# Forgetting attention as a list of steps, with its pieces at fixed places and TensorE in program order

## The chip, the cores and the metric

The kernel runs on one core of a Trainium2 chip. Its engines are TensorE (PE: matrix products; PEld is its weight load), VectorE (DVE), ScalarE (ACT), GpSimd (POOL) and SyncE (SP, which issues DMA transfers). The metric is the time of one execution on the device in microseconds; the figure before is a median of three runs.

## The reference

Two layers work on x of 512 rows by 1024 columns in float32. Each has a SwiGLU feed-forward, a mixer and another feed-forward, all on a normed x and added to it. The mixer of layer 0 is a gated linear recurrence (HGRN2), that of layer 1 the forgetting attention (FoX) of this case:

```
def fox_mixer(h, w_in, b_f, q_norm_g, k_norm_g, w_out):
    q, k, v, g, z_f = split(h @ w_in)              # 16 heads of 64 columns; z_f: one column for each head
    q = rmsnorm(q, q_norm_g);  k = rmsnorm(k, k_norm_g)   # over the 64 columns of a head
    c = cumsum(log_sigmoid(z_f + b_f), axis=rows)
    s = q @ k.T / sqrt(64) + c[query] - c[key]     # only keys at or before the query
    o = softmax(s) @ v
    return (o * sigmoid(g)) @ w_out
```

## The kernel before, in words

Every float32 product is three products: each operand is split into a high part and a rest (`split`, L148: a copy on ScalarE, a subtraction on VectorE), and `mm3` (L167) issues high by high, rest by high and high by rest, at lines 169 to 171. Weights arrive by DMA, are split, and are used once. PSUM has eight banks, given out by kind (L90).

The feed-forwards, and the output projections of both mixers, are written as lists of `Step` objects: a step has `early` work (loads and splits, with a lead in steps), `hooks` (work put ahead of its products), its products `mm`, and `post`. `Line.run` (L293) writes them out one after the other.

The forgetting attention is no such list. `fox` (L868 on) handles the 16 heads in four groups of four, each group as two pairs. For a group it writes, in this order: q and k for all rows (`proj_N`, 96 products of 128x512, tiles `xq..`) with the sums of squares for the norm; the root by a power on GpSimd (`rsqrt_cols`, L177) and the multiplication of q and k by it (`xn`, L998); the values (96 products of 128x256, `xv..`); the gate of the first pair (24 products, `xg..`); the turning of q and k of both pairs by TensorE transposes (`xtp`, L1014) into the stacks QH, QL and KS; the gate of the second pair; and then `attend` for either pair. In group 0 the values' products have 16 more columns, z_f; these are turned (`xzp`, L916) and become c, which goes to DRAM (`cd`) and comes back spread over 128 partitions (`cbc`). `attend` writes the scores for query tiles 3, 2, 1, 0 and both heads (`sc`, two products each, L944 and L945), each followed on VectorE by a pass that adds c and finds the row's extreme (L948), on ScalarE by Exp (L951), and on VectorE by the division (L952, L953). Its `rest` turns the probabilities back (`pT`, L965), copies them (L970 on VectorE, L968 on ScalarE), multiplies them with the values (`xo<-PP,xV`, L973) and applies the gate (L975).

The order in which an engine takes these instructions is not the written one. A scheduler lays the instructions of each engine in order, and puts products of the next group between the pieces of attention of the one before. The `rest` of the last pair is the `late` hook of the output projection, `steps_mix` (L586; xo_ for this mixer, ho_ for the recurrence), which starts when it is written.

Of the kernel before, what the change touches and what calls it, by code (L numbers as in the profile page):

```python
# [12 lines left out]
F32R = mybir.dt.float32r  # L13
# [31 lines left out]
def trunk(ctx: ExitStack, tc: tile.TileContext, a):  # L45
    nc = tc.nc
    MM = nc.tensor.matmul
# [131 lines left out]
    class Norm:  # L179
# [31 lines left out]
        def turn(self, j, kh, kind="turn"):  # L211
# [6 lines left out]
            for kp in range(2):  # L218
                pt = psum(f"{self.id}t{j}{kh}{kp}", (2, H), kind)
                for kk in range(2):  # L220
                    for t in range(2):
                        k = kp * 2 + kk
                        nc.tensor.transpose(pt[:, kk, t * P:(t + 1) * P], self.ys[kh * 2 + t][:, k * P:(k + 1) * P], ident)
# [361 lines left out]
    def steps_mix(nm, src, act, done, late):  # L585

        st = {"w": {}, "b": {}, "bank": {}}

# [9 lines left out]
        def split_b(q):  # L598
            st["b"][q] = split(act(q // 2, 0)[:, q % 2 * 2:q % 2 * 2 + 2, :], B_HL, [2, T], f"{nm}b{q}")

        def mm(half, q, ts, last):
            def what():
                h, l = st["w"]["hl", half, q]
                bh, bl = st["b"][q]
                for t, bank in ts:
                    if q == 0:
                        st["bank"][half, t] = psum(f"{nm}{half}{t}", bank=bank)
                    for kk in range(2):
                        mm3(st["bank"][half, t], bh[:, kk, t * P:(t + 1) * P], bl[:, kk, t * P:(t + 1) * P],
                            h[:, kk, :], l[:, kk, :], q == 0 and kk == 0, q == 3 and kk == 1)  # L610
                if last:
                    drop(bh, bl)
            return what

        def post(half, ts):
# [8 lines left out]
        steps = []  # L624
        for part, (half, ts) in enumerate(((0, ((0, 0), (1, 1), (2, 2))), (1, ((0, 3), (1, 4))),
                                           (1, ((2, 5), (3, 6))), (0, ((3, 7),)))):
            for q in range(4):
                s = Step()
                if part != 2:
                    s.early += [(8, lambda half=half, q=q, part=part: load(half, q, part)), (3, lambda half=half, q=q: split_w(half, q))]  # L630
                if part == 0 and q < 3:
                    s.early.append((3, lambda q=q: split_b(q)))
                elif part == 0:
                    s.hooks += [*late, lambda: split_b(3)]
                s.mm = mm(half, q, ts, part == 3)
                if q == 3:
                    s.post = post(half, ts)
                steps.append(s)
        return steps
# [52 lines left out]
    def hgrn(norm, act, parts):  # L692
# [91 lines left out]
        def states(pr, K, V, tot):  # L784
# [3 lines left out]
            for e in range(2):  # L788
                hs = slice(e * P, (e + 1) * P)
                pk = psum(f"hk{pr}{e}", (NT - 1, P), "ms")  # L790
                for c in range(NT - 1):
                    nc.tensor.transpose(pk[:, c, :], K[:, e, c * P:(c + 1) * P], ident)
# [38 lines left out]
        def finish(pr, ons, gs):  # L831
            for e in range(2):
                h = pr * 2 + e
                pt = psum(f"hot{h}", kind="ms")
                for t in range(NT):
                    nc.tensor.transpose(pt[:, t * P:(t + 1) * P], ons[e][:, t, :], ident)
# [25 lines left out]
    def fox(norm, act, parts):  # L862
        w_in = a["fox_w_in"][0]
        cd = dram.tile([FH, T], F32, name="cd")
        ar0 = turn_of["ar"]
        attended = [0]

# [17 lines left out]
        def values(gr):  # L885

            V = at("ar3", [NT, 256], f"xV{gr}")
            n = 256 + (FH if gr == 0 else 0)
            hs = []
            for q in range(2):  # L890
                w = at("w", [4, 256], f"xv{gr}{q}")
                nc.sync.dma_start(w, w_in[q * 512:(q + 1) * 512, 2 * D + gr * 256:2 * D + gr * 256 + 256].rearrange("(k p) c -> p k c", p=P))
                if gr:
                    hs.append(split(w, W_HL, [4, 256], f"xv{gr}{q}"))
                    drop(w)
                    continue
                h, l = (at("ar", [4, n], f"xv{x}{q}", F32R, slot=ar0 + 2 * q + i) for i, x in enumerate("hl"))
                for cs, raw in ((slice(0, 256), w), (slice(256, n), wz[:, 4 * q:4 * q + 4, :])):
                    nc.scalar.activation(h[:, :, cs], raw, AF.Copy)
                    nc.vector.tensor_sub(l[:, :, cs], raw, r32(h[:, :, cs]))  # L900
                drop(w)
                hs.append((h, l))
            zn = at("y", [NT, FH], "zn") if gr == 0 else None
            for c in range(NT):
                ts = slice(c * P, (c + 1) * P)
                pv = psum(f"xvp{gr}{c}", kind="mm")
                for k in range(NK):
                    h, l = hs[k // 4]
                    mm3(pv[:, :n], norm.cut("h", k, ts), norm.cut("l", k, ts), h[:, k % 4, :], l[:, k % 4, :], k == 0, k == NK - 1)
                nc.scalar.copy(V[:, c, :], pv[:, :256])  # L910
                if gr == 0:
                    nc.scalar.copy(zn[:, c, :], pv[:, 256:n])
            if gr == 0:
                pz = psum("xzp", kind="ms")
                for c in range(NT):
                    nc.tensor.transpose(pz[:FH, c * P:(c + 1) * P], zn[:, c, :], ident)  # L916
                forget(pz[:FH])
            return V

        def attend(gr, pr, stacks, V, sgT):  # L920
            QH, QL, KS = stacks[pr]
            cbs, PPs, sms, mns = [], [], [], []
            for par in range(2):
                h = gr * 4 + pr * 2 + par
                i = attended[0] % 3
                attended[0] += 1
                cb = at(("p1", "p1", "V2")[i], [T], f"cbc{h}", slot=(0, 1, 0)[i])
                nc.sync.dma_start(cb, cd[h:h + 1, :].partition_broadcast(P))
                cbs.append(cb)
                PPs.append(at("ar", [NT, NT, P], f"PP{h}", slot=ar0 + par))  # L930
                both = small(2 * NT, f"mn{h}")
                mns.append(both[:, :NT])
                sms.append(both[:, NT:])
# [3 lines left out]
            for t in reversed(range(NT)):  # L937
                W = (t + 1) * P
                ts_ = slice(t * P, W)
                for par in range(2):  # L940
                    h = gr * 4 + pr * 2 + par
                    cb, PP, mn = cbs[par], PPs[par], mns[par]
                    sc = psum(f"sc{h}{t}", kind="lv")
                    MM(sc[:, :W], lhsT=QH[:, par, ts_], rhs=KS[:, par, :W], start=True, stop=False)  # L944
                    MM(sc[:, :W], lhsT=QL[:, par, ts_], rhs=KS[:, par, :W], start=False, stop=True)  # L945
                    nc.gpsimd.tensor_add(cb[:, ts_], cb[:, ts_], cmask)  # L946
                    row = PP[:, 0:t + 1, t, :]
                    nc.vector.tensor_tensor_reduce(row, cb[:, :W].rearrange("p (b s) -> p b s", s=P),  # L948
                                                   sc[:, :W].rearrange("p (b s) -> p b s", s=P), 1.0, 3.0e38,
                                                   op0=ALU.add, op1=ALU.min, accum_out=mn[:, t:t + 1])  # L950
                    nc.scalar.activation(row, row, AF.Exp, scale=-1.0, bias=mn[:, t:t + 1], accum_out=sms[par][:, t:t + 1])  # L951
                    nc.vector.reciprocal(sms[par][:, t:t + 1], sms[par][:, t:t + 1])  # L952
                    nc.vector.tensor_scalar_mul(row, row, sms[par][:, t:t + 1])  # L953

            drop(QH, QL, KS)

            def rest():
                po = psum(f"xo{gr}{pr}", kind="po")
                for s in range(NT):
                    N = (NT - s) * P  # L960
                    for par in range(2):
                        h = gr * 4 + pr * 2 + par
                        pT = psum(f"pT{h}{s}", kind="ms")
                        for t in range(s, NT):
                            nc.tensor.transpose(pT[:, (t - s) * P:(t - s + 1) * P], PPs[par][:, s, t, :], ident)  # L965
                        PT = PPs[par][:, s, s:, :].rearrange("p t q -> p (t q)")
                        if par:
                            nc.scalar.copy(PT, pT[:, :N])  # L968
                        else:
                            nc.vector.tensor_copy(PT, pT[:, :N])  # L970
                    for par in range(2):
                        rows = slice(par * FD, (par + 1) * FD)
                        MM(po[rows, s * P:], lhsT=V[:, s, (pr * 2 + par) * FD:(pr * 2 + par + 1) * FD],  # L973
                           rhs=PPs[par][:, s, s:, :].rearrange("p t q -> p (t q)"), start=s == 0, stop=s == NT - 1)
                nc.vector.tensor_mul(head_tile(act, gr * 2 + pr), po, sgT[:, pr, :])  # L975
                if pr:
                    drop(sgT)
            return rest

        for gr in range(4):  # L980

            nat = [at("w", [NT, 256], f"xn{gr}{i}") for i in range(2)]
# [188 lines left out]
```

## Time and profile before

| | |
|---|---|
| median of three runs | 2011.36 us (2006.01 to 2011.91) |
| profiled execution | 2011.04 us, span 2009.2 us |
| granted TensorE clock, mean | 0.993 |
| TensorE busy | 1959.0 us, 97% of the span |
| VectorE, ScalarE, GpSimd busy | 1455.6, 1058.2, 261.2 us |
| DMA | 281.40 MB, mean 140 GB/s |

The forgetting attention and its output projection lie between 1342.94 and 1671.52 us of the span. An engine's busy time is the union of its instructions' times; neighbouring matmuls overlap in the trace, so what one costs is read from the distance between two starts.

### The profile page before, as it was taken

The numbers are of one execution on the slowest core, as the hardware profiler recorded it, in microseconds if no ns is written. First come the engines' busy times: TensorE is split into PE (matmuls) and PEld (weight loads), VectorE is DVE, ScalarE is ACT, GpSimd is POOL, SyncE is SP. The second block draws the span as 40 slices with busy tenths as digits, with TensorE's granted clock in tenths as the row PEclk, the third lists the DMA queues.
The fourth block names the chain that finished last, engine by engine and source line by source line (L and its number), as shares of the span: only waits on it lengthen the run. The fifth ranks groups of instructions, "written<-read, shape, count | busy, mean of one in ns | idle before, by whom it ended". The sixth has DMA issues, their size and how long they took to land.

```text
span 2009.2 us, 31752 instructions
## 1 busy us (share of the span) xinstructions
PE 1959.0 (97%) x12821; PEld 1754.9 (87%) x12821; DVE 1455.6 (72%) x1848; ACT 1058.2 (53%) x1595; POOL 261.2 (13%) x249
## 2 busy tenths in 40 slices
PE   6999999999999999999999999999999899999999
PEld 5999987888888899998799999878767668999987
DVE  6767798466565977789797678975566559777796
ACT  6554565432233754556464546567466647444553
POOL 1111211000000011111101110112212200111111
PEclk9999999999999999999999999999999999999999
DMA  6767887221123476785847678672232323767865
GB/s 172 175 154 164 203 186 182 83 63 64 53 85 116 107 178 157 158 227 135 205 110 163 158 162 225 140 176 74 69 91 82 117 63 102 176 154 158 223 149 141
DMA packets 253938, 281.40 MB, mean 140 GB/s; under 512 B 12192, under 2 KB 196944, under 8 KB 253792
## 3 DMA queue, kind: packets, MB, share of 16 engines
q1 hardware_dynamic: 190144, 203.48, 32.3%
q0 software_dynamic: 60576, 75.51, 23.8%
q8 instruction: 100, 1.64, 0.3%
q10 hardware_dynamic: 3072, 0.39, 0.1%
q14 instruction: 46, 0.38, 0.1%
HBM read 277.21 MB, written 2.13 MB: 139 GB/s over the span
## 4 chain that ended last, share of the span: by engine, by line
PE 41%; DVE 4%; ACT 3%; DMA 1%; issue 1%; POOL 0%; POOLq 0%; DVEq 0%; ACTq 0%; SPq 0%
PE f10op L169 2%; PE f10op L170 2%; PE f11op L169 2%; PE f10op L171 2%; PE f11op L170 2%; PE f11op L171 2%; PE xo L973 1%; PE pT L965 1%; PE xvp L171 1%; PE xvp L170 1%; PE xvp L169 1%; PE xo L169 1%; PE xo L171 1%; PE xo L170 1%; DMA f11u4r<-in_ffn_w_in_dram 1%
## 5 line engine op out<-in xcount | busy, mean ns | idle before, releaser
L375 ACT ACTIVATE act<-act 128x512 f32<-128x512 f32 x60 | 37.6, 627 | 55.8 <-DVE act L405 48.5
L946 POOL TENSOR_TENSOR cbc<-cbc,cmask 128x128 f32<-128x128 f32 x64 | 31.6, 496 | 162.4 <-DVE mn L948 112.1
L970 DVE COPY PP<-pT 128x512 f32<-128x512 f32 (+3 forms) x32 | 15.7, 491 | 38.4 <-PE pT L965 38.4
L755 PEld LDWEIGHTS lv<-Q,K 128*128 128x128 f32 x320 | 37.7, 192 | 3.5 <-issue 2.9
L755 PE MATMUL lv<-Q,K 128*128 128x64 f32 x320 | 38.7, 273 | 0.0
L951 ACT ACTIVATE PP<-PP,mn 128x512 f32<-128x512 f32 (+3 forms) x64 | 35.4, 557 | 5.5 <-DVE mn L948 5.0
L965 PEld LDWEIGHTS pT<-ident,PP 128*128 128x128 f32 x160 | 17.7, 145 | 21.6 <-issue 13.4
L968 ACT COPY PP<-pT 128x512 f32<-128x512 f32 (+3 forms) x32 | 13.6, 425 | 40.7 <-PE pT L965 40.7
L948 DVE CUSTOM_DVE_ANT_0 PP<-cbc,sc 128x256 f32<-128x256 f32 (+3 forms) x64 | 30.6, 482 | 6.0 <-PE sc L945 2.9
L165 POOL DMA_DIRECT2D f01ox<-in_ffn_w_out_dram x18 | 20.5, 1143 | 110.0 <-DVE f01op70l L156 31.7
L165 POOL DMA_DIRECT2D f11ox<-in_ffn_w_out_dram x18 | 20.5, 1140 | 107.7 <-DVE f11op70l L156 30.1
L165 POOL DMA_DIRECT2D f00ox<-in_ffn_w_out_dram x18 | 20.4, 1138 | 107.7 <-DVE f00op L472 32.0
L165 POOL DMA_DIRECT2D f10ox<-in_ffn_w_out_dram x18 | 20.5, 1154 | 106.4 <-DVE f10op L472 32.6
L973 PE MATMUL xo<-PP,xV 128*64 128x512 f32 (+3 forms) x128 | 30.8, 467 | 0.0
L944 PE MATMUL sc<-KS,QH 128*128 128x512 f32 (+3 forms) x64 | 23.0, 361 | 7.8 <-DVE mn L948 5.1
L765 DVE TENSOR_TENSOR Q<-Q,tot 128x512 f32<-128x512 f32 x24 | 16.6, 692 | 16.7 <-PE lv L755 10.7
L965 PE MATMUL pT<-ident,PP 128*128 128x128 f32 x160 | 26.7, 294 | 1.3 <-DVE PP L953 1.2
L944 PEld LDWEIGHTS sc<-KS,QH 128*128 128x128 f32 x64 | 12.4, 194 | 16.6 <-DVE mn L948 8.5
L953 DVE TENSOR_SCALAR PP<-PP,mn 128x512 f32<-128x512 f32 (+3 forms) x64 | 25.2, 404 | 1.0
L998 DVE TENSOR_TENSOR xn<-xn,xrr 128x1024 f32<-128x1024 f32 x8 | 9.4, 1223 | 21.3 <-POOL xrr L177 21.3
L945 PE MATMUL sc<-KS,QL 128*128 128x128 f32 (+3 forms) x64 | 21.5, 338 | 0.5 <-ACT QL L1023 0.5
L973 PEld LDWEIGHTS xo<-PP,xV 128*64 128x64 f32 x128 | 9.6, 137 | 13.0 <-DVE PP L970 10.5
(5442 smaller groups left out, 8613.5 us busy)
## 6 DMA issues: line engine op xcount, KB each, us to landing
f00op<-in_ffn_w_out_dram SPq DMA_DIRECT2D x20, 512.0 KB, 4.7
f01op<-in_ffn_w_out_dram SPq DMA_DIRECT2D x20, 512.0 KB, 4.6
f10op<-in_ffn_w_out_dram SPq DMA_DIRECT2D x20, 512.0 KB, 4.6
f11op<-in_ffn_w_out_dram SPq DMA_DIRECT2D x20, 512.0 KB, 4.5
f00ox<-in_ffn_w_out_dram POOLq DMA_DIRECT2D x15, 512.0 KB, 7.8
f01ox<-in_ffn_w_out_dram POOLq DMA_DIRECT2D x15, 512.0 KB, 8.4
f10ox<-in_ffn_w_out_dram POOLq DMA_DIRECT2D x15, 512.0 KB, 7.1
f11ox<-in_ffn_w_out_dram POOLq DMA_DIRECT2D x15, 512.0 KB, 8.3
```

The source lines that it names most:

```text
L165: nc.gpsimd.dma_start(out, in_, accum_op=ALU.add)
L169: MM(out, lhsT=lh, rhs=rh, start=first, stop=False, skip_group_check=more)
L170: MM(out, lhsT=lh, rhs=rl, start=False, stop=False, skip_group_check=more)
L171: MM(out, lhsT=ll, rhs=rh, start=False, stop=last, skip_group_check=more)
L375: nc.scalar.activation(out, out if make else it["A"], AF.Silu)
L755: MM(pl[:, c], lhsT=Kc[:, c, :], rhs=Qv[:, c, :, 1, :], start=True, stop=True)
L944: MM(sc[:, :W], lhsT=QH[:, par, ts_], rhs=KS[:, par, :W], start=True, stop=False)
L946: nc.gpsimd.tensor_add(cb[:, ts_], cb[:, ts_], cmask)
L948: nc.vector.tensor_tensor_reduce(row, cb[:, :W].rearrange("p (b s) -> p b s", s=P), sc[:, :W].rearrange("p (b s) -> p b s", s=P), 1.0, 3.0e38,
L951: nc.scalar.activation(row, row, AF.Exp, scale=-1.0, bias=mn[:, t:t + 1], accum_out=sms[par][:, t:t + 1])
L965: nc.tensor.transpose(pT[:, (t - s) * P:(t - s + 1) * P], PPs[par][:, s, t, :], ident)
L973: MM(po[rows, s * P:], lhsT=V[:, s, (pr * 2 + par) * FD:(pr * 2 + par + 1) * FD], rhs=PPs[par][:, s, s:, :].rearrange("p t q -> p (t q)"), ...
```

## The change

The attention becomes `steps_fox`: 32 steps for each group (16 of q and k, 8 of values, 8 of gates), with loads and splits at a fixed lead. All mixers and feed-forwards from the recurrence's output projection on are one `Line`. The attention of a pair is cut into seven pieces: scores of tile 3, of tile 2, of tiles 1 and 0; then the turning of s=0, that of s=1 with the product of s=0, that of s=2 and 3 with the product of s=1, and the products of s=2 and 3 with the gate. Two more pieces for a group turn q and k of either pair. A table, `PLACES`, names for each piece the step ahead of which it is put, and from the first step of the attention to the middle of the output projection every TensorE instruction is kept in program order. The output projection is cut into smaller steps, for both mixers.

```
+    pe_in_order = [False]
+
+    def MM(*args, **kw):
+        ins = nc.tensor.matmul(*args, **kw)
+        if pe_in_order[0]:
+            tc.keep_in_program_order(ins)
...
+            def rest0():
+                turn(0)
+            def rest1():
+                turn(1)
+                weigh(0)
+            def rest2():
+                turn(2, 3)
+                weigh(1)
+            def rest3():
+                weigh(2)
+                weigh(3)
...
+            return [scores(3), scores(2), scores(1, 0), rest0, rest1, rest2, rest3]
+        return [s for gr in range(4) for s in group(gr)], turned, attend
...
+    fox, turned, attend = steps_fox(n4, act)
+    fox[0].hooks += [lambda: pe_in_order.__setitem__(0, True), lambda: n4.scaled(1)]
...
+    xo, second, split_last = steps_mix("xo_", a["fox_w_out"][0], act, feed(n5), [])
+    xo[second].hooks.append(lambda: pe_in_order.__setitem__(0, False))
+    mid = fox + xo
+    PLACES = (((20, 28), (32, 34, 36, 38, 40, 41, 42), (43, 45, 47, 50, 52, 53, 54)),
...
+    for gr, (turns, *pairs) in enumerate(PLACES):
+        for pr in range(2):
+            mid[turns[pr]].hooks.append(lambda gr=gr, pr=pr: turned(gr, pr))
+            for n, what in zip(pairs[pr], attend(gr, pr)):
+                mid[n].hooks.append(what)
...
-    Line(xo + s3 + o3).run()
+    Line(ho + s1 + o1 + s2 + o2 + fox + xo + s3 + o3).run()
```

On TensorE, the turn of q and k of the last group: `xvp` are values' products, `xg30p` those of the gate of the first pair, `xtp` the transposes. Before, it stands behind all 96 products of values and the 24 of the gate:

```order
L171 MATMUL xvp_15116<-xv31h,n11l_12756 128x256
L169 MATMUL xg30p<-n11h_12749,xg30h 128x512
...
L171 MATMUL xg30p<-n11h_12752,xg30l 128x512
L1014 MATMUL xtp_15180<-ident,xn_14868 128x128 x4
L1014 MATMUL xtp_15193<-ident,xn_14869 128x128 x4
L169 MATMUL xg31p<-n11h_12749,xg31h 128x512
```

After, it stands behind the first 36 products of values:

```order
L50 MATMUL xqp_14958<-xq33sh,n11l_12765 128x512
L50 MATMUL xvp_15023<-xv03sh,n11h_12758 128x256
...
L50 MATMUL xvp_15050<-xv03sh,n11l_12763 128x256
L55 MATMUL xtp_15066<-ident,xn_14815 128x128 x4
L55 MATMUL xtp_15079<-ident,xn_14816 128x128 x4
L50 MATMUL xvp_15050<-xv13sh,n11h_12760 128x256
```

The transposes have moved ahead of 60 products of values and the 24 of the gate; `xqp` is the last product of q and k, from which `xn` is made.

On VectorE, the end of the second pair of group 0: `PP<-pT` are the copies of the turned probabilities (the last two of four are shown), `xn` the multiplication of the next group's q and k by the root, `xss` and `xr1v` what that waits for. Before:

```order
L970 COPY PP_13501<-pT_13598 128x256
L992 TENSOR_REDUCE xss_13619<-xs_13735 128x8
L970 COPY PP_13501<-pT_13608 128x128
L975 TENSOR_TENSOR act_13497<-xo_13571,sgT_13269 128x512
L156 TENSOR_TENSOR xv10l<-xv_13775,xv10h 128x1024
L156 TENSOR_TENSOR xv11l<-xv_13781,xv11h 128x1024
L156 TENSOR_TENSOR xg10l<-xg10w,xg10h 128x1024
L992 TENSOR_REDUCE xss_13619<-xs_13765 128x8
L176 TENSOR_SCALAR xr1v<-xss_13619 128x32
L156 TENSOR_TENSOR xg11l<-xg11w,xg11h 128x1024
L998 TENSOR_TENSOR xn_13617<-xn_13617,xrr_13768 128x1024
L998 TENSOR_TENSOR xn_13618<-xn_13618,xrr_13768 128x1024
```

After:

```order
L166 TENSOR_TENSOR xg11sl<-xg_13800,xg11sh 128x1024
L1142 RECIPROCAL mn_13624<-mn_13624 128x1
L186 TENSOR_SCALAR xr1v<-xss_13483 128x32
L1168 COPY PP_13619<-pT_13771 128x512
L1143 TENSOR_SCALAR PP_13623<-PP_13623,mn_13624 128x128
L1009 TENSOR_TENSOR xn_13481<-xn_13481,xrr_13738 128x1024
L1009 TENSOR_TENSOR xn_13482<-xn_13482,xrr_13738 128x1024
L1168 COPY PP_13619<-pT_13815 128x384
L1168 COPY PP_13619<-pT_13841 128x256
L1168 COPY PP_13619<-pT_13842 128x128
```

The two `xn` have moved from behind all four copies of the probabilities to between the first and the second; a split (`xg11sl`) and two rows of the softmax (`mn`, `PP_13623`) stand ahead of them.

On ScalarE, the Exp of the first pair of group 1. Before, from the gate's Sigmoid (`sgT`) of the second pair on:

```order
L1005 ACTIVATE sgT_13895<-xg11p 128x512
L1023 ACTIVATE QL_13927<-QL_13927 64x512
L155 ACTIVATE xq2s3h<-xq2w_14266 128x1024
L1019 ACTIVATE QH_13951<-xtp_13954,cols 64x512
L1020 ACTIVATE QH_13951<-xtp_13954,cols 64x512
L1025 ACTIVATE KS_13953<-xtp_13967,cols 64x512
L951 ACT_TABLE_LOAD
L951 ACTIVATE PP_14008,mn_14009<-PP_14008,mn_14009 128x4x128
```

After:

```order
L165 ACTIVATE xq22sh<-xq_13972 128x1024
L1141 ACTIVATE PP_13983,mn_13984<-PP_13983,mn_13984 128x4x128
L1141 ACTIVATE PP_13987,mn_13988<-PP_13987,mn_13988 128x4x128
L1054 ACT_TABLE_LOAD
L1054 ACTIVATE sgT_14097<-xgp_13931 128x512
L1141 ACT_TABLE_LOAD
L1141 ACTIVATE PP_13983,mn_13984<-PP_13983,mn_13984 128x3x128
```

One Sigmoid of the gate, which stood ahead of the softmax, stands inside it now, with a table load on either side.

## Rows read from the trace of the kernel before

**Rows 1.** Page, busy time, share of the span and instructions of an engine
```profile
PE 1959.0 (97%) x12821; PEld 1754.9 (87%) x12821; DVE 1455.6 (72%) x1848; ACT 1058.2 (53%) x1595; POOL 261.2 (13%) x249
```
**Rows 2.** Windows: stretch, length, busy of PE, PEld, DVE, ACT, POOL, then clock
```profile
1342.94:1392.54 49.60, 49.36 (x271) 42.06 (x270) 22.93 (x33) 28.25 (x53) 7.17 (x2) 1.00 0.14 42
1392.54:1459.66 67.12, 65.66 (x361) 50.11 (x360) 40.12 (x97) 41.31 (x85) 15.66 (x20) 1.00 0.28 85
1459.66:1526.45 66.79, 65.47 (x361) 50.12 (x360) 40.00 (x97) 41.05 (x85) 14.39 (x17) 1.00 0.32 95
1526.45:1592.81 66.36, 65.09 (x360) 49.71 (x358) 40.61 (x98) 40.74 (x84) 14.30 (x17) 1.00 0.33 104
1592.81:1671.52 78.71, 71.44 (x321) 50.81 (x320) 51.49 (x112) 45.88 (x88) 8.56 (x15) 0.91 0.29 83
```
**Rows 3.** Waits of PE, 1342.94 to 1671.52: total, times, longest (us)
```profile
PE sc L944 <- DVE mn L948: 5.1, 6, 1.5
```
**Rows 4.** Timeline of PE: start, length, engine, line, operation, tiles, shape
```profile
1434.99 0.39 PE L171 MATMUL xq1p<-xq1s3h,n11l 128*128 128x512 f32 x1
...
1435.67 0.39 PE L171 MATMUL xq1p<-xq1s3h,n11l 128*128 128x512 f32 x1
...
1436.01 0.28 PE L170 MATMUL xvp<-xv10l,n11h 128*128 128x256 f32 x1
1436.13 0.28 PE L171 MATMUL xvp<-xv10h,n11l 128*128 128x256 f32 x1
```
**Rows 5.** Timeline of PE, products with the values and transposes of one s
```profile
1409.33 1.35 PE L973 MATMUL xo<-PP,xV 128*64 128x512 f32 x4
1410.62 0.87 PE L965 MATMUL pT<-ident,PP 128*128 128x128 f32 x6
```
**Rows 6.** Timeline, the norm of group 1's q and k
```profile
1436.63 0.62 ACT L991 ACTIVATE xs<-xq1p 128x512 f32<-128x512 f32 x1
...
1438.32 6.42 POOL L177 TENSOR_TENSOR xrr<-xr1v,cols 128x32 f32<-128x32 f32 x1 [12.27 <-ACT xg11h L155]
1444.77 2.36 DVE L998 TENSOR_TENSOR xn<-xn,xrr 128x1024 f32<-128x1024 f32 x2 [5.33 <-POOL xrr L177]
```
**Rows 7.** Timeline, from group 1's turn to its first turned probabilities
```profile
1452.88 1.03 PE L1014 MATMUL xtp<-ident,xn 128*128 128x128 f32 x8
...
1455.71 0.67 ACT L1019 ACTIVATE QH<-xtp,cols 64x512 fp32r<-64x512 f32 x1
...
1461.79 1.06 ACT L155 ACTIVATE xq2s3h<-xq2w 128x1024 fp32r<-128x1024 f32 x1
...
1462.88 1.23 DVE L156 TENSOR_TENSOR xq2s3l<-xq2w,xq2s3h 128x1024 fp32r<-128x1024 f32 x1 [0.65 <-ACT xq2s3h L155]
...
1464.84 1.28 ACT L951 ACT_TABLE_LOAD   x1
...
1466.13 0.72 ACT L951 ACTIVATE PP<-PP,mn 128x512 f32<-128x512 f32 x1
...
1474.63 1.09 PE L965 MATMUL pT<-ident,PP 128*128 128x128 f32 x8 [0.15 <-DVE PP L953]
```
**Rows 8.** Windows, the same stretch (columns as in rows 2)
```profile
1455.71:1474.63 18.92, 17.61 (x82) 13.14 (x80) 14.24 (x40) 18.42 (x38) 2.93 (x6) 1.00 0.36 112
```
**Rows 9.** Timeline, from z_f to the first use of c
```profile
1380.38 0.28 PE L916 MATMUL xzp<-ident,zn 128*16 128x128 f32 x1
...
1393.03 0.46 POOL L946 TENSOR_TENSOR cbc<-cbc,cmask 128x128 f32<-128x128 f32 x1 [16.61 <-DMA cbc<-cd]
```
**Rows 10.** Timeline of PE around a wait in a feed-forward
```profile
986.76 0.40 PE L171 MATMUL f01op<-f01op55h,f01obp52l 128*128 128x512 f32 x1
990.40 0.80 PE L169 MATMUL f01op<-f01op30h,f01obp30h 128*128 128x512 f32 x1 [3.23 <-DVE X L526]
```
**Rows 11.** Windows, behind that wait, and in the last block
```profile
1600.00:1613.80 13.80, 9.62 (x24) 5.12 (x25) 10.32 (x27) 11.22 (x24) 1.86 (x4) 0.51 0.07 24
990.40:996.00 5.60, 5.60 (x13) 4.46 (x14) 3.94 (x4) 2.33 (x6) 1.31 (x1) 0.50 0.07 14
```

More of the change, by code (lines that the diff above doesn't have):

```diff
@@ L596, in split_w, with split_b, mm @@
             drop(w)
[L598 to L601 removed]
+        def split_b(q, kk=None):
+            if q not in st["b"]:
+                st["b"][q] = at(B_HL[0], [2, T], f"{nm}b{q}h", F32R), at(B_HL[1], [2, T], f"{nm}b{q}l", F32R)
+            cut = slice(0, 2) if kk is None else slice(kk, kk + 1)
+            h, l = (x[:, cut, :] for x in st["b"][q])
+            raw = act(q // 2, 0)[:, q % 2 * 2:q % 2 * 2 + 2, :][:, cut, :]
+            nc.scalar.activation(h, raw, AF.Copy)
+            nc.vector.tensor_sub(l, raw, r32(h))
+        def mm(part, q, ts, kks, first, last):
+            half = parts[part][0]
             def what():
@@ L622, in post @@
             return what
[L624 to L638, printed above, removed]
@@ L639, in steps_mix, with piece, weights @@
-        return steps
+        def piece(part, q, ts, kks=(0, 1), first=False, last=False):
+            s = Step()
+            s.mm = mm(part, q, ts, kks, first, last)
+            if last and kks[-1] == 1:
+                s.post = post(part)
+            return s
+        def weights(s, lead, part, q):
+            half = parts[part][0]
+            s.early += [(lead + 4, lambda: load(half, q, part)), (lead, lambda: split_w(half, q))]
+        steps, at_last = [], None
+        for part in (0, 1):
+            for q in range(3):
+                new = [piece(part, q, (t,), first=q == 0) for t in range(len(parts[part][1]))]
+                weights(new[0], 4, part, q)
+                if part == 0:
+                    new[0].early.append((3, lambda q=q: split_b(q)))
+                steps += new
@@ new lines, in steps_mix @@
+        at_last = len(steps)
+        for part in (0, 1):
+            new = [piece(part, 3, range(len(parts[part][1])), (kk,), last=True) for kk in range(2)]
+            weights(new[0], 4, part, 3)
+            steps += new
+        steps[at_last].hooks += late
+        steps[at_last].hooks.append(lambda: split_b(3, 0))
+        steps[at_last + 1].hooks.append(lambda: split_b(3, 1))
+        seconds = len(steps)
+        for n, q in enumerate((1, 2, 3, 0)):
+            steps.append(piece(2, q, (0, 1), first=n == 0, last=n == 3))
+            if q == 0:
+                weights(steps[-1], 2, 2, q)
@@ L642, in load_N @@
+        for q in range(4):
+            steps.append(piece(3, q, (0,), first=q == 0, last=q == 3))
+            weights(steps[-1], 2, 3, q)
+        return steps, seconds, lambda kk: split_b(3, kk)
     def load_N(src, q, cs, nm):
@@ L914, in values, with mm_g, what @@
                 pz = psum("xzp", kind="ms")
                 for c in range(NT):
-                    nc.tensor.transpose(pz[:FH, c * P:(c + 1) * P], zn[:, c, :], ident)
+                    transpose(pz[:FH, c * P:(c + 1) * P], it["zn"][:, c, :], ident)
                 forget(pz[:FH])
[L918 to L939, printed above, removed]
+            def mm_g(half, kk):
+                def what():
+                    if kk == 0:
+                        it["pg", half] = psum(f"xgp{gr}{half}", kind="mm")
+                    h, l = it[f"g{half}"]
+                    for k in (2 * kk, 2 * kk + 1):
+                        mm3(it["pg", half], h[:, k, :], l[:, k, :], norm.cut("h", k), norm.cut("l", k), k == 0, k == NK - 1)
+                return what
@@ L946, in attend @@
[L946 to L959, printed above, removed]
+                    i = attended[0] % 3
+                    attended[0] += 1
+                    cb = at(("p1", "p1", "V2")[i], [T], f"cbc{h}", slot=(0, 1, 0)[i])
+                    nc.sync.dma_start(cb, cd[h:h + 1, :].partition_broadcast(P))
@@ new lines, in turn @@
+            def turn(*ss):
+                if len(ss) == 1:
+                    pts = {(s, par): psum(f"pT{gr}{pr}{s}{par}", kind="ms") for s in ss for par in range(2)}
+                else:
+                    pts = {}
+                    for s in ss:
+                        two = psum(f"pT{gr}{pr}{s}", (2, H), "ms")
+                        pts.update({(s, par): two[:, par, :] for par in range(2)})
+                for s in ss:
+                    for par in range(2):
+                        for t in range(s, NT):
+                            transpose(pts[s, par][:, (t - s) * P:(t - s + 1) * P], at_["PP"][par][:, s, t, :], ident)
+                for s in ss:
@@ L967, in rest @@
                         if par:
-                            nc.scalar.copy(PT, pT[:, :N])
+                            nc.scalar.copy(PT, pts[s, par][:, :N])
                         else:
[L970 to L974, printed above, removed]
```

328 lines of the change are left out of this document (212 added, 116 removed), and 3 rows, old and new, of the table PLACES.

## The prediction

> **What bounds the kernel now.** The page's busy times come first: TensorE is busy for 97% of the span [rows 1]. So the change can gain only where TensorE is slow or idle. I next cut the attention into five windows: the products of group 0, three blocks that each hold the attention of one group and the products of the next, and the attention of group 3 with the output projection [rows 2]. In the three middle blocks TensorE is idle for 1.3 to 1.5 us of 66 to 67; in the last it is idle for 7.3 us, and its granted clock is 0.91. The waits of TensorE over all five are small, the largest sum being 5.1 us for scores that wait for VectorE [rows 3].
>
> Busy time hides what a matmul costs when it runs behind its like, so I took distances between starts. Three products of 128x512 are 0.68 us apart, 0.227 each; 128x256 are 0.12 apart [rows 4]. Eight transposes last 1.09 and six 0.87, so one is 0.11 [rows 5, 7]. The four products of s=0 with the values, in both pieces of 128x512, take 1.29 to the next start [rows 5]; I scale those of s=1, 2, 3 by columns, 3.2 for a pair. Eight pairs of score products are 2.27 by their columns at 0.227. A pair's attention is thus 2.27 + 20 x 0.11 + 3.2 = 7.7.
>
> A group's floor is 96 x 0.227 + 96 x 0.12 + 48 x 0.227 + 16 x 0.11 + 2 x 7.7 = 61.4. The middle blocks are over it by 5.7, 5.4 and 5.0. The last block's is 192 x 0.227 + 32 x 0.11 + 15.4 = 62.6, exceeded by 16.1, most of it in a stretch with the clock at 0.51 [rows 11]. Group 0's products have 48.8, exceeded by 0.8. In all 33.0 us lie above the floor. That is everything that a fixed order could win.
>
> **What the change gives back, part by part.** It removes no arithmetic. The bytes moved are the same; loads keep a lead of 8 or 9 steps of 1.4 us, behind DMA use of about 0.3 [rows 2], so I count nothing for them. The smaller steps of the two output projections are the same products, zero too; in ho_ I bound this by -1 and +1. What it adds is waiting: TensorE in program order stands still when a piece isn't ready, with all products of the next steps queued behind it, where the scheduler's order put those products first.
>
> *Turns.* A turn needs `xn`. From the start of the last q product, 1435.67, through the square, the power on GpSimd (6.42) and the first half of the two passes on VectorE (2.36 for both), `xn` is there after 10.3 us, its second half 1.2 later, of which four transposes cover 0.4 [rows 4, 6]. Before, the turn started 17.2 us after that product [rows 7]. Now, in group 0, one product and 48 of values (0.127 each, by columns) cover 6.3: a wait of 4.0 + 0.7. In group 1, 84 products and four pieces of attention cover 15.5: none. In group 2, 48 products, six transposes and three small products with values cover 8.6: 1.7 + 0.7. In group 3, 36 products cover 4.6: 5.8 + 0.7. Sum 13.6. The lower bound, with the second halves hidden, is 11.5; the upper, with some copies late, 15.
>
> *From the turn to the probabilities.* Before, 21.75 us lie between the first transposes of group 1 and the first turned probabilities [rows 7]. From its first QH on, ScalarE is busy for 18.42 of 18.92 us [rows 8], so this is a chain of work, not slack. It holds splits of 1.06, table loads of 1.28, copies of 0.67, Exps of 0.72 [rows 7]. After, ScalarE's order has the same copies and Exps there, and besides them a Sigmoid with its load between the Exps; with one or two more splits in groups 2 and 3, I take 21.8, 22.8 and 23.9. The cover, in products and pieces that stand between: group 1, 12 x 0.12 + 54 x 0.227 + 1.76 + 2.27 + 0.7 for switching = 18.4; group 2, 48 and 36 products, 18.7; group 3, 60 and 24, 17.4. Short by 3.4, 4.1 and 6.5, in all 14.0. If the chain began only at the first QH, as where ScalarE is free when the turn comes, it is 19.5 and 3.6 are left; with a further load in each, 18. I take 14.0, as the chain's row is the nearest.
>
> The Trainium skill ("ScalarE: Activation LUTs", What ACT_TABLE_LOAD costs) has a switch at about 1283 ns for the load and 1380 ns for a drain. The load is 1.28 here too, but the Exp follows it at once, 1464.84 to 1466.13 [rows 7]: no drain is seen. The attention has six loads more after the change; with drains the sum would be 8.3 higher, about 2032.
>
> *Group 0's c.* From `xzp` to the first addition on `cbc` the trace has 13.1 us, most of it the passes on z, the write of `cd` and its return [rows 9]. Then the softmax follows: 8.5 from the first Exp to the turned probabilities [rows 7], and VectorE's pass ahead of it, taken as long as an Exp, 0.7. The turned probabilities now stand 77 products, eight transposes and 16 score products behind `xzp`: 17.5 + 0.9 + 2.3 = 20.6 against 22.3, a wait of 1.7. Bounds are 0 and 5, the latter with ScalarE shared as in the whole chain above.
>
> *Group 0's second pair.* VectorE now has three splits of 1.23 [rows 7] ahead of the last rows of the softmax, 3.0 with the part that is covered taken off, and both `xn`, which wait for GpSimd's power, ahead of the copy of the second turned probabilities: about 2.0. So 5.0, bounds 0 and 6. Behind that copy on VectorE stand the other copies, and for these wait TensorE's products with the values.
>
> *Insertions.* A middle block's excess of about 5.4 is idle for 1.4 [rows 2]; the other 4.0 go to some 32 changes between products of one kind and another in the written order, 0.13 each. With 14 pieces in a group this stays at 1.8, over four groups 7.3, bounds 5 and 8.
>
> *Clock.* Behind a wait of 3.23 us the granted clock was 0.50 for 5.6 us [rows 10, 11], which holds 14 products at 0.43 instead of 0.227: 2.8 us. The new waits of group 0 and 3 are as long or longer, the others at or below it. I count 2.8 once and 1.0 twice, 4.8; bounds 0 and 17 (six at 2.8).
>
> **Sum.** 13.6 + 14.0 + 1.7 + 5.0 + 7.3 + 4.8 = 46.4 given back, less 33.0 = +13.4. On the profiled execution's 2011.04 (its span of 2009.2 and 1.8 around it), within 0.4 of the median, that is about 2024. With each term at its better or worse bound the two ends would be 1998 and 2047; they will not all fall on one side, and the forecast's own range is 2014 to 2034.
>
> **Rivals.**
>
> *The covers hold.* The softmax chain needs only 19.5 because ScalarE takes it first, c and the second pair come in time, and the clock stays up. Then 13.6 + 3.6 + 5 are given back against 33.0: 2000. For it speaks that the last block alone holds 16.1 us of excess, which fixed pieces spread over 18 steps remove whatever else happens. Against it: ScalarE has no idle time in that stretch [rows 8], and the power's 6.42 us is a fixed price.
>
> *Nothing to be seen.* Turns cost 13.6, but the chains' shortfall is half and the clock falls once: 13.6 + 7 + 1 + 2 + 7 + 2.8 = 33.4, about 2011. For it speaks that the scheduler still places the other four engines' work, and could put the softmax earlier.
>
> *The clock falls at every wait.* Six waits at 2.8 instead of 4.8 in all: 2036. The row for it is the one behind 3.23 us, and the last block, which has several waits of 1 to 1.5 us [rows 3] and then a clock of 0.51 [rows 11]. That speaks for it, since no single wait there is as long as 3 us; against it, each new wait is followed by dense products. The Trainium skill ("TensorE: Matmul & The Clock Gate", HAM oscillation) has a throttled time cost half of itself; half of the 5.6 us is 2.8, and the row agrees.
>
> That the order isn't what the change says is no rival, since TensorE's rows show each piece at its place.
>
> **How the numbers follow.** A run of this kernel can't be told from no change within about 0.3%, 6 us. I give the forecast 0.50, the covers that hold 0.19, no change 0.17, the clock 0.14. Faster is the first rival, 0.19. Same is the second and the low tail of the forecast, below 2017, 0.05: 0.22. Slower is the rest, 0.59. The range goes from 2003, which leaves out about half of the first rival, to 2038, which leaves out about half of the third.
>
> **What would show it.** Right: in the changed kernel's trace, waits of TensorE for `xn` at the turns of groups 0, 2 and 3 of 2 to 7 us each with GpSimd's power behind them; waits for `PP` at the first turned probabilities of groups 1, 2 and 3 of 3 to 7 us; the clock below 1 in the windows behind the longest; and the last block down to 65 to 75 us. Wrong: if ScalarE has idle time in the softmax stretch, or the waits for `PP` are under 1 us, the chain was over-estimated and the time falls to 2000; if the last block doesn't fall below 75, its excess isn't of the order's making, and the time is above 2030.

## The result, and the profile after

The changed kernel takes 2028.51 us (median of four runs) where the kernel before takes 2009.28: a ratio of 1.0092, interval 1.0077 to 1.0108. It is slower by 0.9%, about 18.5 us. The prediction said 2024, in 2003 to 2038, slower. In the profiled execution (2027.82 us, span 2026.1) the attention starts at 1342.60 and its output projection ends at 1688.20: 345.6 us, where the sum of [rows 2] is 328.6. The other 17 us begin and end there; the rest of the program is as it was.

The windows of the changed kernel, cut at the first scores of each group as those of [rows 2] (columns the same):

```profile
1342.60:1398.41 55.81, 50.83 (x276) 44.12 (x277) 25.19 (x35) 31.43 (x57) 7.63 (x3) 0.97 0.23 68
1398.41:1467.80 69.39, 59.88 (x332) 47.55 (x331) 40.44 (x98) 41.04 (x87) 15.32 (x20) 0.95 0.31 93
1467.80:1532.10 64.30, 60.50 (x343) 48.95 (x343) 37.63 (x96) 40.38 (x84) 13.30 (x17) 0.97 0.22 67
1532.10:1605.90 73.80, 65.06 (x350) 52.36 (x350) 40.45 (x97) 41.60 (x84) 16.05 (x17) 0.93 0.25 81
1605.90:1688.20 82.30, 77.37 (x374) 60.54 (x374) 53.84 (x113) 49.82 (x91) 10.81 (x15) 0.96 0.31 94
```

TensorE's idle time has gone from 1.3 to 1.5 us in a middle block to between 3.8 and 9.5, and the clock, which was 1.00 in the first four blocks, is below 1 in all. TensorE's waits in this stage (total, times, longest):

```profile
PE xtp L55 <- DVE xn L1009: 11.5, 5, 5.8
PE pT L55 <- DVE PP L1143: 9.8, 5, 2.5
PE xtp L55 <- DVE QL L1087: 5.7, 3, 3.6
PE sc L50 <- DVE mn L1138: 2.9, 3, 1.3
PE pT L55 <- DVE PP L1168: 1.1, 1, 1.1
PE xtp L55 <- DVE KS L1092: 0.5, 3, 0.2
```

That is 31.5 us, against 11.0 in the same stage before, of which [rows 3] are the largest. There was none for `xn` there, and those for `QL` at a turn and for `PP` were small:

```profile
PE xtp L1014 <- DVE QL L1021: 1.6, 4, 0.6
PE pT L965 <- DVE PP L953: 1.2, 2, 1.0
```

The turn of group 3 shows the first of them whole (timeline):

```profile
1587.40 0.18 DVE L186 TENSOR_SCALAR xr3v<-xss 128x32 f32<-128x32 f32 x1
1587.73 6.42 POOL L187 TENSOR_TENSOR xrr<-xr3v,cols 128x32 f32<-128x32 f32 x1 [14.59 <-ACT xg13sh L165]
1594.18 2.36 DVE L1009 TENSOR_TENSOR xn<-xn,xrr 128x1024 f32<-128x1024 f32 x2 [5.33 <-POOL xrr L187]
...
1595.55 2.16 PE L55 MATMUL xtp<-ident,xn 128*128 128x128 f32 x8 [5.78 <-DVE xn L1009]
```

The same power of 6.42 us as in [rows 6] is now followed by TensorE standing still. Two of the other waits are a second turn (group 1; VectorE's `QL`, which reads what the first turn left, stands behind ScalarE's copy `QH`) and first turned probabilities (group 2):

```profile
1461.36 0.76 DVE L1087 SCALAR_TENSOR_TENSOR QL<-xtp,cols,QH 64x512 fp32r<-64x512 f32 x1 [0.83 <-ACT QH L1086]
1462.26 0.63 PE L55 MATMUL xtp<-ident,xn 128*128 128x128 f32 x4 [3.64 <-DVE QL L1087]
...
1545.67 0.69 PE L55 MATMUL pT<-ident,PP 128*128 128x128 f32 x2 [2.55 <-DVE PP L1143]
```

Three windows give what else runs: ScalarE during these two waits, and the clock behind the wait of group 3.

```profile
1542.90:1545.67 2.77, 0.22 (x1) 0.00 (x1) 1.74 (x10) 2.50 (x9) 0.12 (x1) 0.93 0.74 226
1458.40:1462.26 3.86, 0.22 (x1) 0.03 (x1) 2.60 (x4) 3.65 (x6) 0.00 (x0) 1.00 0.66 165
1595.40:1603.00 7.60, 7.04 (x40) 6.33 (x41) 4.14 (x6) 6.07 (x10) 0.00 (x0) 0.71 0.00 0
```

ScalarE is busy for 2.50 of 2.77 us in the one and 3.65 of 3.86 in the other; behind 5.8 us of standing still the clock is 0.71 over 7.6 us.

### The profile page after: what moved, and what is told of

Read it like the earlier page. It is cut to its first block, busy times and chain, and to the rows that moved or that the text cites. A ratio compares the mean times of both kernels' runs of the same rounds, so it can differ in the third digit from the quotient of the medians.

```text
span 2026.1 us, 31758 instructions
## 1 busy us (share of the span) xinstructions
PE 1953.1 (96%) x12821; PEld 1763.1 (87%) x12821; DVE 1458.4 (72%) x1852; ACT 1066.6 (53%) x1605; POOL 264.5 (13%) x249
## 3 DMA queue, kind: packets, MB, share of 16 engines
q8 instruction: 100, 1.64, 0.3%
## 4 chain that ended last, share of the span: by engine, by line
PE 38%; DVE 5%; DMA 3%; ACT 2%; issue 1%; POOL 1%; POOLq 0%; ACTq 0%; DVEq 0%; SPq 0%
PE f11op L50 5%; PE xqp L50 4%; PE f10op L50 4%; PE xo L50 3%; POOL xrr L187 1%; PE xgp L50 1%; PE xvp L50 1%; PE pT L55 1%; PE f01op L50 1%; PE sc L50 1%; DMA f10u4r<-in_ffn_w_in_dram 1%; PE f11u3A L50 1%; PE f11g3A L50 1%; PE f11u2A L50 1%; PE f11g2A L50 1%
## 5 line engine op out<-in xcount | busy, mean ns | idle before, releaser
L1136 POOL TENSOR_TENSOR cbc<-cbc,cmask 128x128 f32<-128x128 f32 x64 | 36.1, 568 | 193.9 <-DVE mn L1138 129.4
L50 PEld LDWEIGHTS lv<-Q,K 128*128 128x128 f32 (+2 forms) x512 | 45.7, 165 | 6.2 <-issue 5.3
L50 PE MATMUL lv<-Q,K 128*128 128x64 f32 (+2 forms) x512 | 47.6, 248 | 0.0
L1141 ACT ACTIVATE PP<-PP,mn 128x512 f32<-128x512 f32 (+3 forms) x64 | 35.4, 554 | 18.9 <-DVE mn L1138 18.5
L1138 DVE CUSTOM_DVE_ANT_0 PP<-cbc,sc 128x512 f32<-128x512 f32 (+3 forms) x64 | 29.7, 480 | 11.8 <-PE sc L50 9.7
L1168 DVE COPY PP<-pT 128x512 f32<-128x512 f32 (+3 forms) x32 | 14.9, 487 | 28.4 <-PE pT L55 28.4
L175 POOL DMA_DIRECT2D f01ox<-in_ffn_w_out_dram x18 | 20.5, 1142 | 110.5 <-DVE f01op L482 31.5
L809 DVE TENSOR_TENSOR Q<-Q,tot 128x512 f32<-128x512 f32 x24 | 16.6, 692 | 16.6 <-PE lv L50 16.4
L55 PE MATMUL xtp<-ident,xn 128*128 128x128 f32 x64 | 11.2, 311 | 17.6 <-DVE xn L1009 11.5
L1143 DVE TENSOR_SCALAR PP<-PP,mn 128x512 f32<-128x512 f32 (+3 forms) x64 | 26.4, 421 | 1.2
L55 PEld LDWEIGHTS xtp<-ident,xn 128*128 128x128 f32 x64 | 7.8, 155 | 20.5 <-issue 12.4
L1087 DVE SCALAR_TENSOR_TENSOR QL<-xtp,cols,QH 64x512 fp32r<-64x512 f32 x16 | 12.0, 749 | 16.4 <-ACT QH L1086 15.3
L50 PE MATMUL xo<-PP,xV 128*64 128x512 f32 (+3 forms) x128 | 22.5, 452 | 0.0
```

The costliest lines, as they stand in the source:

```text
L50: ins = nc.tensor.matmul(*args, **kw)
L55: ins = nc.tensor.transpose(*args)
L175: nc.gpsimd.dma_start(out, in_, accum_op=ALU.add)
L809: nc.vector.tensor_mul(Qh[:, :, 1, :], Qh[:, :, 1, :], tv[:, :, 0:1].to_broadcast([P, nb_, m]))
L1143: nc.vector.tensor_scalar_mul(row, row, sm[:, t:t + 1])
L1168: nc.vector.tensor_copy(PT, pts[s, par][:, :N])
```

## The experiments

The theory was that the fixed places put the turns ahead of the norm and the turned probabilities ahead of ScalarE's work; the rivals, that the fixed order itself costs, or that what is gained at one wait is lost at the next. Ratios are to the kernel before.

**The places kept, the order free.** `pe_in_order` is never set.

```
-    fox[0].hooks += [lambda: pe_in_order.__setitem__(0, True), lambda: n4.scaled(1)]
+    fox[0].hooks += [lambda: n4.scaled(1)]
```

> The changed kernel with the same steps, pieces and places, but TensorE's order left to the scheduler. Theory (the places themselves are too early for this chip's norm and softmax, whoever sets the order): the scheduler fills only the waits that its own estimate shows. In its order the second turn of group 1 and two first turned probabilities stand behind more products than before (waits of 4.0 and 2 to 3 us go), while the turn of group 0 stands 11 products earlier (1.4 us more wait): about 2023 us, a turn of group 0 that still waits 4 to 7 us. Rival (the fixed program order is what costs): the waits for xn and PP fall to those of the kernel before, 2010 us.

Measured: 2013.54 us, ratio 1.0023 (1.0014 to 1.0033). Its waits:

```profile
PE xtp L55 <- DVE xn L1009: 10.6, 4, 5.5
PE pT L55 <- DVE PP L1143: 3.7, 5, 1.5
PE pT L55 <- DVE PP L1168: 2.8, 1, 2.8
...
PE xtp L55 <- DVE QL L1087: 1.1, 2, 0.7
```

Both theories had half. The waits for `xn` stay, so the scheduler does not seem to foresee them (group 0's turn stands behind the same 48 products of values; that it had moved by 11 was misread from the order). Those for `QL` and `PP`, L1143 and L1168 together, fall from 16.6 to 7.6, since products go in front. So a free order takes back most of the loss by filling a part of the waits; it stays some 4 us above the kernel before.

**The norm cut in four, multiplication and all.** Root and multiplication for each row tile as it comes, in either kernel:

```
-                    if c == NT - 1:
-                        rr = small(NT * 8, f"xrr{gr}")
-                        rsqrt_cols(rr, it["ss"].rearrange("p c h -> p (c h)"), NT * 8, 1.0 / FD, f"xr{gr}")
...
+                    nc.gpsimd.tensor_tensor(it["rr"][:, cs], it["rv"][:, cs], nhalf[:, :8], op=ALU.pow)
+                    for i in range(2):
+                        n4 = it["nat"][i][:, c].rearrange("p (h d) -> p h d", d=FD)
...
+                        nc.vector.tensor_mul(n4, n4, r4.unsqueeze(2).to_broadcast([P, 4, FD]))
```

> The changed kernel with the root of the norm and the multiplication by it done for each row tile of q and k as it comes, 8 columns at a time, instead of 32 columns at the end. The power takes 6.4 us for 32 columns and 1.0 for 4, so about 1.6 for 8; xn is ready some 5 us earlier. Theory (the turns wait for the norm): TensorE's waits for xn of 5.0, 3.1 and 6.1 us in groups 0, 2 and 3 shrink to under 1 each, and less time is at the low clock: 13 to 16 us less, about 2013. Rival (ScalarE's softmax work bounds the stretch, and the wait moves on to the probabilities): the waits for PP grow by what those for xn shrink, 2024 or more.

> The kernel before with the same edit of the norm's root. There the turn stands 17.2 us behind the last q product and the norm needs 10.3: theory, 5 us less of it change nothing, within 2 us of the kernel before. Rival (the norm is on the path there too): 10 us or more faster.

Measured: 2025.45 in the changed kernel, ratio 1.0084 (1.0062 to 1.0105), and 2019.05 in the kernel before, 1.0055 (1.0034 to 1.0077): slower there, which no theory had. The waits for `xn` do go, but others come. In the changed kernel:

```profile
PE pT L55 <- DVE PP L1145: 14.7, 9, 2.5
...
PE xtp L55 <- DVE xn L1011: 1.2, 2, 0.9
```

and in the kernel before, by its waits and its timeline on VectorE:

```profile
PE xo L973 <- DVE PP L970: 10.6, 9, 1.8
```

```profile
1426.43 1.30 DVE L1001 TENSOR_TENSOR xn<-xn,xrr 128x256 f32<-128x256 f32 x2 [1.54 <-POOL xrr L997]
1427.66 0.68 DVE L970 COPY PP<-pT 128x512 f32<-128x512 f32 x1
```

The small multiplications stand in VectorE's queue and wait there for GpSimd; the copy of the turned probabilities stands behind them, and TensorE's product with the values waits for that copy.

**The power alone cut in four.** As above, but both multiplications whole and at the end, again in either kernel.

```
+                    if c == NT - 1:
+                        rr = it["rr"]
...
+                            nc.vector.tensor_mul(n4, n4, r4.unsqueeze(3).to_broadcast([P, NT, 4, FD]))
```

> The changed kernel with only the power on GpSimd cut in four: 8 columns after each row tile, so that after the last tile 8 columns (1.6 us) are left instead of 32 (6.4). The two multiplications by the root stay whole and at the end, so that VectorE's queue holds nothing new that waits for GpSimd. Theory (the turns wait for the norm; what spoilt the first cut of the norm is the eight small multiplications that stand in VectorE's queue ahead of copies and softmax rows): the waits for xn of groups 0, 2 and 3 fall from 5.0, 1.0 and 6.1 to under 1.5 each, the copies of the second pair of group 0 come 4 us earlier, 10 to 14 us less in all, about 2016. Rival (whatever comes earlier is lost at the probabilities): the waits for PP rise to 18 us as in the first cut, 2024.

> The kernel before with only the power cut in four and both multiplications whole at the end. Theory: there the norm is hidden behind values and gate, and the first cut of the norm was slow in that kernel for its eight small multiplications alone; this one is within 3 us of the kernel before, so that what the spaced places win is the places' and not the norm's. Rival (the cut itself is worth something in any order): 5 us or more faster.

Measured: 2014.56 in the changed kernel, ratio 1.0027 (1.0016 to 1.0037), 14 us less than without; 2011.37 in the kernel before, 1.0012 (1.0001 to 1.0022), no gain. So the norm's length costs where the turn is fixed early, and nothing where it comes late; and what made the first cut slow in the kernel before were its small multiplications. In the changed kernel:

```profile
PE pT L55 <- DVE PP L1147: 9.8, 5, 2.5
PE xtp L55 <- DVE QL L1091: 5.5, 2, 3.6
...
PE xtp L55 <- DVE xn L1013: 3.0, 3, 2.0
```

Waits for `xn` fell by 8.5; those for `PP` of L1143 and for `QL` stayed. Of the copies of group 0's second pair only the 1.1 us for L1168 went, not the wait ahead of them. The rest of the 14 us is less time above a product's floor, with the clock over the stage at 0.97 instead of 0.96.

**Places later.** First turns three, two and three steps later in groups 0, 2 and 3, and the pieces behind them with them in groups 2 and 3:

```
-    PLACES = (((20, 28), ...), ..., ((84, 86), (88, 90, 92, 94, ...)...), ((115, 117), (119, 121, 122, 124, ...)...))
+    PLACES = (((23, 28), ...), ..., ((86, 88), (90, 92, 94, 96, ...)...), ((118, 120), (122, 124, 125, 127, ...)...))
```

> The changed kernel with other places: the first turn of groups 0, 2 and 3 comes 3, 2 and 3 steps of values later (1.44 us each), and in groups 2 and 3 the pieces behind it 2 to 3 steps later too, so that the cover from turn to probabilities stays what it was. Theory: the waits for xn of 5.0, 3.1 and 6.1 become 0.7, 0.3 and 1.7, those for PP stay within 1 us: 11 to 14 us less with the clock, about 2016. Rival (what follows the norm is bound by ScalarE from an earlier point, so a later turn makes a later softmax): the waits for PP grow, 2025 or more.

Measured: 2011.37, ratio 1.0011 (1.0001 to 1.0022): 17 us less, without any change in what is computed or in the fixed order. The waits for `xn` went from 11.5 to 1.3; those at the second turns grew.

```profile
PE xtp L55 <- DVE QL L1087: 9.1, 3, 3.6
PE pT L55 <- DVE PP L1143: 7.0, 5, 2.4
...
PE xtp L55 <- DVE xn L1009: 1.3, 2, 0.8
```

**Second turns later.** In groups 1, 2 and 3, from 57, 86 and 117 to 60, 89 and 120; nothing else.

> The changed kernel with the second turns of groups 1, 2 and 3 put three steps later, nothing else moved. The trace has the second turn of group 1 wait 4.0 us and that of group 2 2.1 us for QL, that is for a PSUM bank that the first turn's copies on ScalarE still read. Theory: these two waits go, and the copies of the second turn stand behind the first Exps on ScalarE: about 6 us less, 2022. Rival (ScalarE's work between the turn and the probabilities is the bound, in whatever order): the waits for PP take them over, 2027.

Measured: 2026.80, ratio 1.0089 (1.0074 to 1.0104). The rival had it. The waits for `QL` are gone and those for `PP` are 5.5 us longer; while TensorE stands in the longest of them, in group 1, ScalarE is busy for 4.73 of 4.80 us:

```profile
PE pT L55 <- DVE PP L1143: 15.3, 5, 4.1
PE xtp L55 <- DVE xn L1009: 11.2, 5, 5.8
```

```profile
1474.50:1479.30 4.80, 0.72 (x4) 0.30 (x3) 3.56 (x19) 4.73 (x15) 1.02 (x2) 0.79 0.35 111
```

**All places moved at once,** in fixed and in free order: first turns at 26, 55, 86 and 118, second turns at 30, 60, 91 and 123, pieces behind them 2 to 4 steps later in groups 2 and 3.

> Places that answer to every wait seen: first turns of groups 0, 2 and 3 at 26, 86 and 118 instead of 20, 84 and 115; second turns at 30, 60, 91 and 123; in groups 2 and 3 the pieces behind them 2 to 4 steps later. Theory: against the run with later places (2011) the wait of xzp for zn (2.2 us), those of the second turns (4.0, 3.0, 3.0) and two of those for PP (2.1, 1.6) go, with part of the time at the low clock: 2000 to 2004, below the kernel before. Rival (they move on to the probabilities): 2010.

> The same places, but TensorE's order left to the scheduler, which may put other products into a wait that it foresees. Theory (with good places the fixed order has little to lose): within 3 us of the run with the fixed order. Rival (the fixed order itself costs, since it can't fill the small waits): 5 us or more faster than that.

Measured: 2021.46, ratio 1.0066 (1.0051 to 1.0081), and 2008.56, 1.0000 (0.9991 to 1.0009). In the fixed order both the theory and its rival missed; of the free order the rival was right. In the fixed one the waits for `PP` rose to 16.0 and a turn of group 0 waited for the one just before it (`KS`, 4.1):

```profile
PE pT L55 <- DVE PP L1143: 16.0, 5, 4.7
PE xtp L55 <- DVE KS L1092: 4.1, 1, 4.1
```

A fixed order is only as good as each of its places, and I had moved the turns towards the probabilities they feed. The free order was 13 us better on the same places.

**The gate without its Sigmoid.** A copy stands in its place.

> The changed kernel with the attention's gate left without its Sigmoid: ScalarE copies the gate's products instead, so the output lacks the Sigmoid, and the loads of its table and of Exp's behind it go, up to 1.28 us each, in the stretch from turn to probabilities of groups 1 to 3. Theory (ScalarE's work bounds that stretch): the waits for PP of 1.1, 2.9 and 4.8 us at the first turned probabilities shrink by 1.3 to 2.6 us each, about 6 us less, 2022. Rival (something else, VectorE's queue or GpSimd's additions, bounds it): no change, 2028.

Measured: 2018.14, ratio 1.0049 (1.0034 to 1.0064), 10 us less than the changed kernel. The waits for `PP` fell only from 9.8 to 7.2:

```profile
PE pT L55 <- DVE PP L1143: 7.2, 3, 2.4
```

Those of group 1 and the second of group 3 (1.86) are gone, but the one of group 2 is 2.41 after 2.55. The window of this wait shows what holds it now: VectorE is busy for all of it, with a split of weights (`xq23sl`, 1.21 us) between the divisions, and ScalarE for 0.77.

```profile
1540.30:1542.71 2.41, 0.00 (x1) 0.00 (x1) 2.41 (x10) 0.77 (x4) 0.00 (x0) 1.00 0.63 223
```

So ScalarE's loads bound the stretch in part, with VectorE's queue close behind them. The stage is 8.3 us shorter, of which the waits are 2.7; the rest goes with a clock of 0.97 over the stage instead of 0.96.

**Spaced places.** The power cut in four and, with it, first turns at 21, 54, 85 and 116, and 12 or 13 steps instead of 9 or 10 from a turn to the first turned probabilities in groups 1 to 3; in fixed and in free order.

```
+ ((54, 58), (59, 61, 63, 67, 69, 70, 71), (72, 74, 76, 79, 81, 82, 83)),
+ ((85, 89), (90, 92, 94, 98, 100, 101, 102), (103, 105, 107, 110, 112, 113, 114)),
+ ((116, 120), (121, 123, 124, 128, 130, 131, 132), (133, 134, 135, 138, 140, 141, 142))
```

> The power cut in four (as in the run that left 8 columns for the end) with places to suit: first turns at 21, 54, 85 and 116, second turns 4 steps behind (7 in group 0), and 12 or 13 steps instead of 9 or 10 from a turn to the first turned probabilities in groups 1 to 3, some 4.1 us more of products. Theory (only more products between turn and probabilities cover ScalarE's work there; a later second turn alone does not): of the 5.1, 5.1 and 7.0 us that groups 1, 2 and 3 still waited in that run, about 4 us each go: 2002 to 2005, faster than the kernel before. Rival (the work moved towards the end of the attention makes the last pair late in the output projection): 2010.

> The same kernel as the one with the spaced places and the cut power, but TensorE's order left to the scheduler. Theory (the order by itself costs only where the places leave a wait that the scheduler sees, 13 us with the places all moved): with fewer waits the two lie within 4 us of each other, both at or below the kernel before: 1999 to 2005. Rival (the fixed order costs its 13 us whatever the places): this one 2000 or less and the fixed one 2010 or more.

Measured: 1998.95, ratio 0.9949 (0.9932 to 0.9965), and 1991.72, 0.9916 (0.9900 to 0.9932). Both beat the kernel before, and the fixed one by more than forecast. The free order is 7 us better still, more than the theory's 4 and less than the rival's 10: it fills part of what is left. Against the kernel with the power alone cut (2014.56) the fixed one differs in its places only, and these are worth 15.6 us. The attention and its projection in the one and in the other:

```profile
1344.00:1660.11 316.11, 304.41 (x1668) 244.87 (x1669) 197.62 (x450) 203.61 (x399) 65.64 (x84) 0.99 0.29 89
```

```profile
1343.58:1655.22 311.64, 303.94 (x1670) 243.38 (x1669) 198.10 (x450) 203.33 (x400) 66.10 (x84) 1.00 0.30 91
```

In the fixed one the waits at the turns are gone but for 0.2. Of the two largest sums that are left most is group 0's (2.4 for `PP`, 2.0 for `mn`); new are four waits for the splits of the next group's weights, 3.4 us, of which the longest is shown last:

```profile
PE pT L55 <- DVE PP L1147: 3.3, 3, 2.4
PE sc L50 <- DVE mn L1142: 3.0, 4, 1.1
PE xqp L50 <- ACT xq32sh L165: 1.6, 1, 1.6
```

ScalarE and VectorE are as busy as in the changed kernel (203.6 and 197.6 us); besides the shorter power only the products that stand between a turn and its use are other ones.

## Why the prediction was right

*The floor and the excess.* The stage has 295.6 of floor; 345.6 is 50.0 above it, where 33.0 + 13.4 = 46.4 was forecast. Of this the waits are 31.5, for which the four terms of waits gave 34.3; the rest is 18.5, where insertions and clock were to be 12.1 (before, the rest is 328.6 - 295.6 - 11.0 = 22.0).

*Turns:* forecast 13.6, measured 11.5. The gaps ahead of the first turns of groups 0 and 3 came as computed (3.9 and 0.6 in group 0 for 4.0 and 0.7; 5.8 in group 3 for 5.8), that of group 2 was 1.2 for 2.4, outside the 2 to 7 us that the prediction gave as a sign. Cutting the power and moving the places each took most of this term away alone (3.0 and 1.3 are left).

*From turn to probabilities:* forecast 14.0, to be met as 3 to 7 us at the first turned probabilities of groups 1 to 3 each. Measured there are 0.7, 2.6 and 2.3, with 1.9 behind them in group 3, so 7.4 (9.8 less group 0's); and 5.7 at the second turns, which the prediction did not have at all: their transposes wait for `QL`, and this for ScalarE's copies. Together they are 13.1, and the run with the second turns later shows that they are one wait, which goes from the one place to the other. So the step had the right bound and missed where TensorE first meets it, and the sign that less than 1 us means a short chain misled in group 1. The size is in part luck: from a turn to the turned probabilities the trace has 24.7, 25.5 and 23.6 us for 21.8, 22.8 and 23.9 forecast, and without the waits in between some 20 to 21 of cover for 17.4 to 18.7, two errors that nearly cancel. (Its lower bound is mis-added: a chain of 19.5 leaves 4.0 over these covers, not 3.6.)

*Group 0:* its second pair waited 2.4 and 1.1, 3.5 for a forecast of 5.0. For c, two waits for `mn` come to 2.2 for a forecast of 1.7, at the scores and not at the turned probabilities.

*Insertions and clock* are where the sum was out, 18.5 for 12.1, and the mis-sized term is the clock. Each block's length times what its clock lacks of 1 in the rows above adds up to 15.5 us, a part of it while TensorE stood still anyway; product by product, the trace has it busy for 26 us at half the clock, which cost 13, where 4.8 was forecast. I had counted three places, and the clock is below 1 in all five blocks; the third rival's 16.8 was nearer. (The 5.6 us that the term was priced by hold 13 products [rows 11], not 14: 2.6 instead of 2.8.) What is left for insertions is some 5 of the 7.3 forecast. In the kernel before, the same reckoning leaves 17 (33.0 less 11.0 of waits and 5 of clock). So the fixed order did win some 12 us between the products, and lost more than that in waits (20) and clock (8). That 2024 came within 5 us of the result owes something to errors that went opposite ways: the clock's by 8, the insertions' and the waits' by 2 and 3.

*The last block* was to fall to 65 to 75 us and is 82.3. The prediction held that this would put the time above 2030 and show that the block's excess isn't of the order's making; neither follows, since the two windows don't hold the same work. Behind the first scores of group 3 there now stand 12 products of values and 48 of the gate that stood ahead of them before, and 374 products instead of 321 [rows 2]. With the prediction's prices for what each window holds, the floor is 61.6 before (the prediction had 62.6) and 73.1 now, and the excess falls from 17.1 to 9.2. In the spaced kernel, with a floor of 70.3, it is 4.0 and the clock is 1.00:

```profile
1585.86:1660.11 74.25, 72.53 (x355) 55.62 (x355) 53.50 (x115) 49.70 (x91) 8.49 (x15) 1.00 0.37 112
```

*Table loads.* The sum with a drain after each, by the Trainium skill ("ScalarE: Activation LUTs", What ACT_TABLE_LOAD costs), was 2032, not far from the result. But the trace again shows none: in the changed kernel a load of 1.28 at 1540.34 is followed by its Sigmoid at 1541.63.

```profile
1540.34 1.28 ACT L1054 ACT_TABLE_LOAD   x1
1541.63 0.60 ACT L1054 ACTIVATE sgT<-xgp 128x512 f32<-128x512 f32 x1
```

Of the rivals, the one in which the covers hold (2000) needed other places and a shorter power: the spaced kernel, 1999, is that case.

## What to carry to other kernels

Where pieces are put at fixed places, work out for each the longest chain that feeds it on the other engines, from traced durations, and count the products that stand in between: here 10.3 us for the norm and 24 to 26 from turn to probabilities. Some waits go when one place is moved, as those for the norm did. A wait that comes of an engine's work over a whole stretch does not: it turned up at the next piece that needs the same engine, until more products stood between the chain's start and its end. An instruction that waits for a third engine should stand late in its queue, whatever its size. And before two windows are compared, count whether they hold the same work.

## What was not expected of the hardware

A power on GpSimd took 5.44 or some 6.4 us for 32 columns: the same instruction, on the same shape, came out 1 us longer in two of the four groups of the changed kernel, and in all four of the kernel before. Of 8 columns it took 1.65 in most cases, but in the changed kernel with the power alone cut four of the sixteen took 2.7; one of each is shown. Idle time ahead of it does not decide: in the spaced kernel one took 1.64 after 8.77 us of it. What sets the extra microsecond was not tried.

```profile
1567.73 1.65 POOL L1007 TENSOR_TENSOR xrr<-xrv,cols 128x8 f32<-128x8 f32 x1 [3.13 <-DVE xrv L1006]
1577.81 2.70 POOL L1007 TENSOR_TENSOR xrr<-xrv,cols 128x8 f32<-128x8 f32 x1 [8.43 <-DVE xrv L1006]
```
